# A log-softmax over rows of 50000: one product per tile in place of four, and a subtraction shared by two engines

## The chip, the cores and the metric

The kernel runs on one core of a Trainium2 chip. A core has a matrix engine (TensorE, PE in the profile), a vector engine (VectorE, DVE), a scalar engine (ScalarE, ACT), GpSimd (POOL) and SyncE (SP), which only issues transfers here. Sixteen DMA engines move data between the core's on-chip memory and the chip's main memory; their transfers are issued from SP (loads) and from ScalarE's queue (stores). The metric is the device time of one execution in microseconds (us), the median of several.

## What is computed

```python
batch, seq, vocab = 16, 512, 50000
max_x = np.max(x, axis=-1, keepdims=True)
shifted = x - max_x
log_sum_exp = np.log(np.sum(np.exp(shifted), axis=-1, keepdims=True))
return (shifted - log_sum_exp).astype(np.float32)
```

There are 8192 rows of 50000 numbers in float32. Each row is read once and written once.

## The kernel before

A tile is 32 rows. Each row lies on four neighbouring partitions (`G = 4`), so a tile fills 128 partitions with 12500 columns each (`W`), 50000 bytes on a partition. There are 256 tiles and four buffers for them (`NBUF = 4`, `bufs`); tile t uses buffer t mod 4. A tile is read into its buffer, changed in place and stored from there. For some steps the columns are taken in four pieces of 3125 (`NS`, `C`, `cols(c)`).

The order of work is written out by hand, engine by engine, with semaphores between the engines. There is no scheduler. `Count` (L35 and on) numbers the events of a semaphore, and `take` (L47) waits for a transfer and lowers its semaphore again. Most tiles run in a hardware loop of four tiles a round, with the first and last four outside on VectorE and the last four outside on ScalarE and TensorE.

- SP loads. The first four tiles are loaded at once (the first in two halves). After that the load of tile t + 4 waits at `take` until the store of tile t has landed (L158 to L161).
- VectorE, for a tile: wait until it has landed (L201); four maxima over 3125 columns each, negated, into `negm` (L206); the smallest of the four, `negp` (L211); then `share`, two transposes with a reduction and a copy between them (L171 to L186), which makes the four partitions of a row agree on one maximum, `negmax`. When ScalarE has its scales, VectorE multiplies them with the four partial sums, `scaled` (L217), and, when the logarithm is there, it subtracts maximum and logarithm from the whole tile in place (L191). Only the last tile is subtracted in four pieces.
- ScalarE, for a tile: after each of the four maxima, the exponential of that piece with its own maximum, summed into `part` (L248), the exponentials themselves being thrown away in `dump`; the four scales that bring the partial sums to the common maximum (L256); the logarithm of the row sum (L239); and then the issue of the tile's store, which waits until VectorE has subtracted (L243). Behind a store on this queue stand the next tile's exponentials. The last tile is stored in four pieces (L278 and L279).
- TensorE adds up: four products of the constant matrix `ones` (1 where two partitions belong to the same row) with the four columns of `scaled`, accumulated into one column of `sums` (L285).

In short, for one tile: load, maxima (with the exponentials behind them), agreement, scales, `scaled`, products, logarithm, subtraction, store.

Of the kernel before, what the change touches and what calls it, by code (L numbers as in the profile page):

```python
# [9 lines left out]
ACT = mybir.ActivationFunctionType  # L10
ALU = mybir.AluOpType
AX = mybir.AxisListType.X
# [6 lines left out]
C = 3125  # L19
NBUF = 4  # L20

NS = 4

HEAD = 2

# [19 lines left out]
def take(engine, sem, n=16):  # L45

    engine.wait_ge(sem, n).then_inc(sem, -n)  # L47


def cols(c):  # L50
    return slice(c * C, (c + 1) * C)
# [3 lines left out]
def kernel(  # L55
# [9 lines left out]
    W = V // G  # L65
    assert N % R == 0 and W == NS * C
    ntiles = N // R
# [6 lines left out]
    ot = of.rearrange("(t r) (g w) -> t (r g) w", r=R, g=G)  # L74

    def run(a, first, n):

        part = a[first : first + NBUF * n].rearrange("(q i) p w -> q i p w", i=NBUF)
        return lambda q, i: part[bass.ds(q, 1), i].rearrange("o p w -> (o p) w")
# [12 lines left out]
    ones = consts.tile([P, P], FP32, name="ones")  # L92
    bufs = [data.tile([P, W], FP32, name=f"buf{j}") for j in range(NBUF)]
    dump = dump_pool.tile([P, C], FP32, name="dump")
    sums = sum_pool.tile([P, NBUF], FP32, name="sums")
    rowsums = [sums[:, k : k + 1] for k in range(NBUF)]

    def each(n, width, name):
        return [stats.tile([P, width], FP32, name=f"{name}{j}") for j in range(n)]

    negms, parts, scales, scaleds = (
        each(NBUF, NS, n) for n in ("negm", "part", "scale", "scaled")
    )
    negmaxs, logs = each(NBUF, SQ, "negmax"), each(NBUF, 1, "logsum")
    (negp,) = each(1, 1, "negp")
    (allneg,) = each(1, SQ, "allneg")
    (rowneg,) = each(1, SQ // G, "rowneg")
# [5 lines left out]
    def sem(name):  # L113
        return ctx.enter_context(nc.semaphore(name))

    landed = [sem(f"landed{j}") for j in range(NBUF)]
    stored = [sem(f"stored{j}") for j in range(NBUF)]
    heads = [sem(f"head{h}") for h in range(HEAD)]
    ready = sem("ones_ready")
    on_dve = Count(sem("on_dve"))  # L120
    on_act = Count(sem("on_act"))
    shifted = Count(sem("shifted"))
    agreed = Count(sem("agreed"))
    rescaled = Count(sem("rescaled"))
    summed = Count(sem("summed"))
    added = Count(sem("added"))
    logged = Count(sem("logged"))
    subtracted = Count(sem("subtracted"))

    block = ctx.enter_context(nc.Block())  # L130

    @block.gpsimd
    def _(gpsimd):
        view = ones.rearrange("p (r g) -> p r g", g=G)
        gpsimd.memset(ones, 1.0).then_inc(ready)  # L135
        gpsimd.affine_select(  # L136
            out=view, in_=view, pattern=[[-G, R], [0, G]], base=0,
            channel_multiplier=1, compare_op=ALU.is_ge, fill=0.0,
        ).wait_op(ready, 1, "sem-ge").then_inc(ready)
        gpsimd.affine_select(  # L140
            out=view, in_=view, pattern=[[G, R], [0, G]], base=G - 1,
            channel_multiplier=-1, compare_op=ALU.is_ge, fill=0.0,
        ).wait_op(ready, 2, "sem-ge").then_inc(ready)

    @block.sync
    def _(sync):
# [15 lines left out]
        for j in range(NBUF - 1):  # L162
            take(sync, stored[j])
        take(sync, stored[NBUF - 1], 16 * NS)

    @block.vector
    def _(vector):
        def share(k):

            on_dve.next(  # L170
                vector.transpose(out=allneg, in_=negp.to_broadcast([P, SQ]))  # L171
            ).then_inc(on_dve.sem)
            on_dve.next(
                vector.tensor_reduce(  # L174
                    out=rowneg, in_=allneg.rearrange("p (r g) -> p r g", g=G),
                    op=ALU.min, axis=AX,
                )
            ).then_inc(on_dve.sem)
            on_dve.next(
                vector.tensor_copy(  # L180
                    out=spread.rearrange("p (r g) -> p r g", g=G),
                    in_=rowneg[:, :, None].to_broadcast([P, SQ // G, G]),
                )
            ).then_inc(on_dve.sem)
            on_dve.next(
                vector.transpose(out=negmaxs[k], in_=spread)  # L186
            ).then_inc(agreed.sem)

        def subtract(k, *bufs):
            for n, buf in enumerate(bufs):  # L190
                ins = vector.tensor_scalar(  # L191
                    out=buf, in0=buf, scalar1=negmaxs[k][:, 0:1], scalar2=logs[k],
                    op0=ALU.add, op1=ALU.subtract,
                )
                if n == 0:
                    logged.next(ins)
                ins.then_inc(subtracted.sem)

        def whole(j, first=False, by_pieces=False):
            if not first:  # L200
                take(vector, landed[j])  # L201

            for c in range(NS):
                if first and c % (NS // HEAD) == 0:
                    take(vector, heads[c // (NS // HEAD)])
                vector.tensor_reduce(  # L206
                    out=negms[j][:, c : c + 1], in_=bufs[j][:, cols(c)],
                    op=ALU.max, axis=AX, negate=True,
                ).then_inc(shifted.sem if c < NS - 1 else on_dve.sem)
            on_dve.next(vector.nop()).then_inc(shifted.sem)  # L210
            vector.tensor_reduce(  # L211
                out=negp, in_=negms[j], op=ALU.min, axis=AX
            ).then_inc(on_dve.sem)
            share(j)

            rescaled.next(
                vector.tensor_mul(out=scaleds[j], in0=scales[j], in1=parts[j])  # L217
            ).then_inc(summed.sem)
            subtract(j, *([bufs[j][:, cols(c)] for c in range(NS)] if by_pieces else [bufs[j]]))

        def settle():
            for count in (on_dve, rescaled, logged):
                count.settle(vector)

        for j in range(NBUF):
            whole(j, first=j == 0)
        settle()
        with vector.Fori(0, rounds - 1):
            for j in range(NBUF):
                whole(j)  # L230
            settle()
        for j in range(NBUF):
            whole(j, by_pieces=j == NBUF - 1)

    @block.scalar
    def _(scalar):
        def log(k):
            added.next(
                scalar.activation(out=logs[k], in_=rowsums[k], func=ACT.Ln)  # L239
            ).then_inc(logged.sem)  # L240

        def store(j, dst, buf):
            subtracted.next(scalar.dma_start(out=dst, in_=buf)).then_inc(stored[j], 16)  # L243

        def whole(j):
            for c in range(NS):
                shifted.next(
                    scalar.activation(  # L248
                        out=dump, in_=bufs[j][:, cols(c)], func=ACT.Exp,
                        bias=negms[j][:, c : c + 1], scale=1.0,  # L250
                        accum_out=parts[j][:, c : c + 1],
                    )
                ).then_inc(on_act.sem)
                on_act.next(scalar.nop())  # L254
            agreed.next(
                scalar.activation(  # L256
                    out=scales[j], in_=negms[j], func=ACT.Exp,
                    bias=negmaxs[j][:, 0:1], scale=-1.0,
                )
            ).then_inc(rescaled.sem)  # L260
            log(j)

        def settle():
            for count in (on_act, shifted, agreed, added, subtracted):
                count.settle(scalar)

        nc.scalar.preload_act_table_set("natural_log_exp_and_others")  # L267
        dst = run(ot, 0, rounds)
        with scalar.Fori(0, rounds) as q:
            for j in range(NBUF):  # L270
                whole(j)
                store(j, dst(q, j), bufs[j])
            settle()
        for j in range(NBUF - 1):
            whole(j)
            store(j, ot[ntiles - NBUF + j], bufs[j])
        whole(NBUF - 1)
        for c in range(NS):  # L278
            store(NBUF - 1, ot[ntiles - 1][:, cols(c)], bufs[NBUF - 1][:, cols(c)])  # L279

    @block.tensor
    def _(tensor):
        def whole(j):
            for c in range(NS):
                ins = tensor.matmul(  # L285
                    rowsums[j], ones, scaleds[j][:, c : c + 1],
                    start=c == 0, stop=c == NS - 1,
                )
                if c == 0:
                    summed.next(ins)  # L290
            ins.then_inc(added.sem)

        tensor.wait_ge(ready, 3)
        with tensor.Fori(0, rounds):
            for j in range(NBUF):
                whole(j)
            summed.settle(tensor)
        for j in range(NBUF):
            whole(j)
# [30 lines left out]
```

## Time and profile before

| what | value |
|---|---|
| median of 3 runs | 7586.61 us (7581.52 to 7590.15) |
| the profiled execution's own time | 7610.41 us |
| its span in the profile | 7608.7 us |
| VectorE busy | 5441.5 us, 72% |
| ScalarE busy | 3184.7 us, 42% |
| TensorE busy | 477.9 us, 6% (2048 records) |
| bytes moved | 3276.85 MB, mean 431 GB/s |
| maximum over 3125 columns (L206), 1024 of them | 3401 ns each |
| exponential over 3125 columns (L248), 1024 of them | 2868 ns each |
| subtraction over 12500 columns (L191) | 6791 ns each |
| product of `scaled` (L217), 128x4 | 163 ns each |
| minimum of four columns (L211), 128x4 | 157 ns each |
| load of a tile, 6250 KB, issue to landing | 44.2 us, median |
| store of a tile, 6250 KB, issue to landing | 47.9 us, median |

An engine's busy time leaves out its waits and the issue of transfers. One product of `ones` with a column of float32 appears as two records of weights and two of the product itself, hence 2048 records for 256 x 4 products. The busy times of the engines overlap in time, so they are not to be added.

### The profile page before, as it was taken

The page shows a single profiled execution, that of the slowest core. Times are in us where ns is not written, and L with a number is a line of the kernel's source. Part 1 is how long each engine was busy: PE and PEld are TensorE (multiplying, and loading weights), DVE is VectorE, ACT ScalarE, POOL GpSimd, SP SyncE. Part 2 cuts the span into 40 slices and gives each one's busy share as a digit, 9 for nine tenths or more (in the row PEclk, how much of TensorE's full clock was granted, in tenths as well). Part 3 has the DMA queues.
Part 4 walks back from the last instruction along what each step waited for, and adds up shares of the span by engine and source line. Part 5 has one row for each costly group of instructions (what it writes and reads, how often), then busy time and mean ns, then how long its engine had stood idle before and what let it go on. Part 6 is the DMA issues. An engine that isn't in the chain of part 4 may idle for free. (4 is left out here: it accounts for less than half of the span.)

```text
span 7608.7 us, 14069 instructions
## 1 busy us (share of the span) xinstructions
PE 477.9 (6%) x2048; PEld 456.0 (6%) x2048; DVE 5441.5 (72%) x2819; ACT 3184.7 (42%) x2561; POOL 1.4 (0%) x7
## 2 busy tenths in 40 slices
PE   0000000000000000000000000000000000000000
PEld 0000000000000000000000000000000000000000
DVE  7777777767777777777777777777777777777776
ACT  4444443443434444344443444434344443443443
POOL 0000000000000000000000000000000000000000
DMA  9999999999999999999999999999999999999999
GB/s 425 435 434 433 433 432 433 432 430 433 435 434 433 433 432 431 433 433 433 433 431 433 433 432 432 433 430 433 431 432 433 430 432 427 430 428 430 431 429 387
DMA packets 74307, 3276.85 MB, mean 431 GB/s; under 512 B 8257, under 2 KB 8257, under 8 KB 8257
## 3 DMA queue, kind: packets, MB, share of 16 engines
q1 hardware_dynamic: 37008, 1638.42, 50.2%
q10 hardware_dynamic: 37296, 1638.42, 49.8%
q14 instruction: 3, 0.02, 0.0%
HBM read 1638.40 MB, written 1638.40 MB: 431 GB/s over the span
## 5 line engine op out<-in xcount | busy, mean ns | idle before, releaser
L248 ACT ACTIVATE dump<-buf,negm 128x3125 f32<-128x3125 f32 x1024 | 2937.3, 2868 | 3828.4 <-DVE negm L206 3730.9
L206 DVE TENSOR_REDUCE negm<-buf 128x1 f32<-128x3125 f32 x1024 | 3418.4, 3401 | 946.4 <-DVEq L47 946.4
L191 DVE TENSOR_SCALAR buf<-buf,negmax,logsum 128x12500 f32<-128x12500 f32 (+1 forms) x259 | 1739.0, 6715 | 553.7 <-ACT logsum L239 553.7
L285 PE MATMUL sums<-scaled,ones 128*128 128x1 f32 x2048 | 477.9, 355 | 7110.7 <-DVE scaled L217 7110.7
L285 PEld LDWEIGHTS sums<-scaled,ones 128*128 128x128 f32 x2048 | 456.0, 328 | 7132.6 <-DVE scaled L217 7132.6
L217 DVE TENSOR_TENSOR scaled<-scale,part 128x4 f32<-128x4 f32 x256 | 41.7, 163 | 579.9 <-ACT scale L256 579.9
L239 ACT ACTIVATE logsum<-sums 128x1 f32<-128x1 f32 x256 | 43.8, 171 | 551.1 <-PE sums L285 551.1
L248 ACT ACTIVATION_READ_ACCUMULATOR dump<-buf,negm 128x1 f32 x1024 | 190.9, 186 | 0.0
L256 ACT ACTIVATE scale<-negm,negmax 128x4 f32<-128x4 f32 x256 | 76.1, 297 | 23.6
L211 DVE TENSOR_REDUCE negp<-negm 128x1 f32<-128x4 f32 x256 | 40.2, 157 | 39.2 <-DVE negm L206 39.2
L186 DVE STREAM_TRANSPOSE negmax<-spread 128x32 f32<-128x32 f32 x256 | 54.2, 212 | 8.9
L171 DVE STREAM_TRANSPOSE allneg<-negp 128x32 f32<-128x32 f32 x256 | 54.2, 212 | 8.9
L174 DVE TENSOR_REDUCE rowneg<-allneg 128x8 f32<-128x32 f32 x256 | 47.7, 186 | 8.9
L180 DVE COPY spread<-rowneg 128x32 f32<-128x32 f32 x256 | 46.5, 182 | 8.9
L267 ACT ACT_TABLE_LOAD x1 | 1.3, 1283 | 1.0 <-SPq L111 1.0
L136 POOL TENSOR_SCALAR_AFFINE_SELECT ones<-ones 128x128 f32<-128x128 f32 x1 | 0.5, 518 | 0.1
L140 POOL TENSOR_SCALAR_AFFINE_SELECT ones<-ones 128x128 f32<-128x128 f32 x1 | 0.5, 517 | 0.1
L135 POOL MEMSET ones<- 128x128 f32 x1 | 0.2, 204 | 0.5 <-SPq L111 0.5
L314 POOL MEMSET const-bfloat16-1.0<- 128x1 bf16 x1 | 0.1, 101 | 0.0
L314 POOL MEMSET const-uint8-127<- 128x1 uint8 x1 | 0.1, 101 | 0.0
L314 POOL MEMSET const-float32-0.0<- 128x1 f32 x1 | 0.1, 98 | 0.3 <-issue 0.3
L314 POOL MEMSET const-float32-1.0<- 128x1 f32 x1 | 0.1, 98 | 0.0
## 6 DMA issues: line engine op xcount, KB each, us to landing
buf<-in_x_dram SPq DMA_DIRECT2D x255, 6250.0 KB, 44.2
out_dram<-buf ACTq DMA_DIRECT2D x255, 6250.0 KB, 47.9
buf<-in_x_dram SPq DMA_DIRECT2D x2, 3125.0 KB, 14.0
out_dram<-buf ACTq DMA_DIRECT2D x4, 1562.5 KB, 8.1
```

Source lines behind the costliest of these rows:

```text
L171: vector.transpose(out=allneg, in_=negp.to_broadcast([P, SQ]))
L174: vector.tensor_reduce(out=rowneg, in_=allneg.rearrange("p (r g) -> p r g", g=G), op=ALU.min, axis=AX,)
L180: vector.tensor_copy(out=spread.rearrange("p (r g) -> p r g", g=G), in_=rowneg[:, :, None].to_broadcast([P, SQ // G, G]),)
L186: vector.transpose(out=negmaxs[k], in_=spread)
L191: ins = vector.tensor_scalar(out=buf, in0=buf, scalar1=negmaxs[k][:, 0:1], scalar2=logs[k], op0=ALU.add, op1=ALU.subtract,)
L206: vector.tensor_reduce(out=negms[j][:, c : c + 1], in_=bufs[j][:, cols(c)], op=ALU.max, axis=AX, negate=True,).then_inc(shifted.sem if c < ...
L211: vector.tensor_reduce(out=negp, in_=negms[j], op=ALU.min, axis=AX).then_inc(on_dve.sem)
L217: vector.tensor_mul(out=scaleds[j], in0=scales[j], in1=parts[j])
L239: scalar.activation(out=logs[k], in_=rowsums[k], func=ACT.Ln)
L248: scalar.activation(out=dump, in_=bufs[j][:, cols(c)], func=ACT.Exp, bias=negms[j][:, c : c + 1], scale=1.0, accum_out=parts[j][:, c : c + 1],
L256: scalar.activation(out=scales[j], in_=negms[j], func=ACT.Exp, bias=negmaxs[j][:, 0:1], scale=-1.0,)
L285: ins = tensor.matmul(rowsums[j], ones, scaleds[j][:, c : c + 1], start=c == 0, stop=c == NS - 1,)
```

## The change

TensorE's four products per tile become one: VectorE first adds the four columns of `scaled` into one column, `totals`, and that is multiplied with `ones`. The subtraction of a tile is divided by columns. VectorE subtracts the first three quarters (9375 columns, `OWN`) as before. For the last quarter VectorE computes `offsets`, the negated maximum less the logarithm, in one column, and ScalarE adds it to the last 3125 columns in place with an Identity activation whose bias is that column. The store of a tile now waits for both: a no-operation on ScalarE waits for its own Identity, and the store itself for VectorE. On the last tile VectorE subtracts three pieces, and the four stores wait one by one for their own piece, the fourth for the Identity. The full diff but for the new counters and lists:

```diff
+OWN = (NS - 1) * C
...
+    totals = each(NBUF, 1, "total")
+    offsets = each(NBUF, 1, "offset")
...
+    offset = Count(sem("offset"))
+    shared = Count(sem("shared"))
...
         def subtract(k, *bufs):
-            for n, buf in enumerate(bufs):
-                ins = vector.tensor_scalar(
+            logged.next(
+                vector.tensor_sub(out=offsets[k], in0=negmaxs[k][:, 0:1], in1=logs[k])
+            ).then_inc(offset.sem)
+            for buf in bufs:
+                vector.tensor_scalar(
                     out=buf, in0=buf, scalar1=negmaxs[k][:, 0:1], scalar2=logs[k],
                     op0=ALU.add, op1=ALU.subtract,
-                )
-                if n == 0:
-                    logged.next(ins)
-                ins.then_inc(subtracted.sem)
+                ).then_inc(subtracted.sem)
...
             rescaled.next(
                 vector.tensor_mul(out=scaleds[j], in0=scales[j], in1=parts[j])
+            ).then_inc(on_dve.sem)
+            on_dve.next(
+                vector.tensor_reduce(
+                    out=totals[j], in_=scaleds[j], op=ALU.add, axis=AX
+                )
             ).then_inc(summed.sem)
-            subtract(j, *([bufs[j][:, cols(c)] for c in range(NS)] if by_pieces else [bufs[j]]))
+            own = [cols(c) for c in range(NS - 1)] if by_pieces else [slice(0, OWN)]
+            subtract(j, *(bufs[j][:, part] for part in own))
...
         def store(j, dst, buf):
+            shared.next(scalar.nop())
             subtracted.next(scalar.dma_start(out=dst, in_=buf)).then_inc(stored[j], 16)
...
             log(j)
+            offset.next(
+                scalar.activation(
+                    out=bufs[j][:, OWN:], in_=bufs[j][:, OWN:], func=ACT.Identity,
+                    bias=offsets[j], scale=1.0,
+                )
+            ).then_inc(shared.sem)
...
         for c in range(NS):
-            store(NBUF - 1, ot[ntiles - 1][:, cols(c)], bufs[NBUF - 1][:, cols(c)])
+            count = shared if c == NS - 1 else subtracted
+            count.next(
+                scalar.dma_start(
+                    out=ot[ntiles - 1][:, cols(c)], in_=bufs[NBUF - 1][:, cols(c)]
+                )
+            ).then_inc(stored[NBUF - 1], 16)
...
         def whole(j):
-            for c in range(NS):
-                ins = tensor.matmul(
-                    rowsums[j], ones, scaleds[j][:, c : c + 1],
-                    start=c == 0, stop=c == NS - 1,
-                )
-                if c == 0:
-                    summed.next(ins)
-            ins.then_inc(added.sem)
+            summed.next(
+                tensor.matmul(rowsums[j], ones, totals[j], start=True, stop=True)
+            ).then_inc(added.sem)
```

## The prediction

> **What bounds the kernel now.** I read first the page's slices, because they say whether any engine or the DMA engines are full all the way; then the waits, to see who is late; then one tile of the timeline; then the end of the span in windows.
>
> The page, its slices (each a fortieth of the span, 190 us) and its queues:
>
> ```profile
> span 7608.7 us, 14069 instructions
> DVE  7777777767777777777777777777777777777776
> ACT  4444443443434444344443444434344443443443
> DMA  9999999999999999999999999999999999999999
> GB/s 425 435 434 433 433 432 433 432 430 433 435 434 433 433 432 431 433 433 433 433 431 433 433 432 432 433 430 433 431 432 433 430 432 427 430 428 430 431 429 387
> q1 hardware_dynamic: 37008, 1638.42, 50.2%
> q10 hardware_dynamic: 37296, 1638.42, 49.8%
> ```
>
> VectorE is busy seven tenths of the time, ScalarE four. The two DMA queues, loads (q1) and stores (q10), take 50.2% and 49.8% of 16 engines' time: together all of it. The rate is flat at 427 to 435 GB/s from the second slice to the last but one; only the ends drop. The work is 3276.85 MB, which no edit of the change touches.
>
> The list of waits (who waited for whom: us in total, times, longest):
>
> ```profile
> ACT dump L248 <- DVE negm L206: 3730.9, 768, 15.3
> DVE negm L206 <- DVEq L47: 946.4, 253, 11.7
> DVE scaled L217 <- ACT scale L256: 579.9, 256, 2.3
> DVE buf L191 <- ACT logsum L239: 553.7, 256, 2.2
> ```
>
> The second line decides. L47 is `take`, VectorE's wait for a tile to land, and it came last 253 times of 256. The engines wait for data; they are not what data waits for. One tile of the timeline (start, duration, engine, work, idle before it and releaser):
>
> ```profile
> 7527.32 0.16 DVE L217 TENSOR_TENSOR scaled<-scale,part 128x4 f32<-128x4 f32 x1 [2.26 <-ACT scale L256]
> 7527.53 1.87 PE L285 MATMUL sums<-scaled,ones 128*128 128x1 f32 x8 [27.64 <-DVE scaled L217]
> 7529.44 0.17 ACT L239 ACTIVATE logsum<-sums 128x1 f32<-128x1 f32 x1 [2.15 <-PE sums L285]
> 7529.64 6.79 DVE L191 TENSOR_SCALAR buf<-buf,negmax,logsum 128x12500 f32<-128x12500 f32 x1 [2.16 <-ACT logsum L239]
> 7536.47 0.35 ACTq L243 DMA_DIRECT2D out_dram<-buf  x1
> 7539.97 3.41 DVE L206 TENSOR_REDUCE negm<-buf 128x1 f32<-128x3125 f32 x1 [3.53 <-DVEq L47]
> ```
>
> After its store is issued VectorE stands idle 3.53 us. The next tile's subtraction begins at 7559.15 in the same view, 29.51 us after this one. A tile moves 6250 KB each way, 12.8 MB; at 433 GB/s that is 29.56 us. So the period is the DMA's, and the compute of a tile is 29.51 - 3.53 = 26.0 us of it.
>
> The end, in windows (us, busy time of PE, its weight load, DVE, ACT and POOL, clock, DMA share of 16 engines, GB/s):
>
> ```profile
> 7500.00:7558.00 58.00, 2.83 (x13) 2.74 (x13) 42.51 (x22) 24.80 (x20) 0.00 (x0) 1.00 1.00 429
> 7567.00:7580.00 13.00, 0.00 (x0) 0.00 (x0) 10.30 (x4) 6.21 (x5) 0.00 (x0) 1.00 1.00 431
> 7582.00:7590.00 8.00, 1.87 (x8) 1.78 (x8) 3.28 (x8) 4.22 (x6) 0.00 (x0) 1.00 0.06 25
> 7592.00:7606.00 14.00, 0.00 (x0) 0.00 (x0) 4.24 (x3) 0.00 (x0) 0.00 (x0) 1.00 1.02 429
> ```
>
> The share of 0.06 is one engine of sixteen. One DMA engine lags behind the others and is still storing tile 254 while the rest idle before tile 255's pieces, whose first store is issued at 7590.82. It has hardly a gap of its own, so it sets the end.
>
> **What the Trainium skill says.** "DMA: Bandwidth & Descriptors", section "Where 436 GB/s comes from", puts the ceiling of a core's 16 DMA engines at 435.2 GB/s; the page's 430 to 435 agrees, there is nothing left above it. "SBUF — State Buffer", section "Who interferes with whom", says that DMA never contends with a compute engine. The trace agrees as far as it can: 13 us with only stores and a busy VectorE ran at 431 GB/s, 14 us with VectorE mostly idle at 429. "ScalarE: Activation LUTs", section "What ACT_TABLE_LOAD costs", gives 280 ns + 0.833 ns an element for an ACTIVATE with a bias of one value per partition, whatever the function: 2883 ns for 3125 columns; the exponential of that width takes 2868 here. "VectorE: DVE Perf Modes", section "Mode 2×_2P — use both read ports for one tensor", allows two elements a cycle for an odd width if source and destination have the same; the trace has such an odd case, the last tile's 3125 columns at about 1.9 us, against 3.4 us for a maximum over as many.
>
> **The change part by part.** Times are per tile, from the product on VectorE (L217) on.
>
> Products: the eight PE records of a tile take 1.87 us, of 355 ns each by the page, so their starts lie (1.87 - 0.355) / 7 = 0.22 us apart. Two remain: 0.22 + 0.355 = 0.57 us. Gain 1.30.
>
> New sum over four columns (`totals`): nearest row the minimum over four columns at L211, 157 ns, and about 0.03 us of start. Cost 0.19; bounds 0.16 and 0.25.
>
> New `offsets`: a 128x1 subtraction, nearest row L217's 163 ns, plus 0.03 between instructions. It stands on VectorE ahead of the large subtraction. Cost 0.2; bounds 0.1 and 0.25.
>
> Large subtraction: 12500 columns take 6.79 us, 3125 take 1.84 (7.36 over four). Between them (6.79 - 1.84) / 9375 = 0.528 ns a column, so 9375 columns take 1.84 + 6250 x 0.528 = 5.14 us. Gain 1.65. If the odd width fell to one element a cycle, at the maximum's 3.4 us per 3125 it would be about 10.2 us: a loss of 3.4.
>
> ScalarE's Identity on 3125 columns: 2.87 us, bounds 2.8 and 3.3, since it writes to SBUF where the exponential writes to PSUM. It begins when the offset is there, beside VectorE's 5.14 us, so it ends some 2.2 us before and hides. Behind it on ScalarE stand the new no-operation that waits for it, the store, and the next tile's exponentials, which could not start sooner than a landing and a maximum later anyway. SP's loads wait only for stores.
>
> Sum: the chain from landing to store loses 1.30 + 1.65 - 0.19 - 0.2 = 2.56 us, 26.0 to 23.4. Over 256 tiles that is 655 us of compute taken away, and none of it lies on the path: the next tile has not landed. VectorE's wait at `take` grows from 3.5 to about 6.1 us, in total from 946 to 946 + 253 x 2.56 = about 1590 us. The store enters a DMA queue earlier and stays in it that much longer. The first loop rounds, where tiles follow without a wait at L47, gain nothing either: DMA is full from 2.2 us on (426 GB/s up to 60 us).
>
> Only the end is not covered by DMA. There the last tile's first piece is issued earlier by 1.30 - 0.19 - 0.2 = 0.9 us, provided that its DMA issue passes the Identity that runs ahead of it on ScalarE; if it doesn't, the issue follows Identity, 2.87 instead of 1.9 us after the offset, and the net is nothing. The later three pieces have a DMA engine to wait for in either case. And the lagging engine is busy with tile 254 until about 7591.6, so a gain stops at about 0.7. I take 0.5.
>
> Against the profiled execution: 7610.4 (span 7608.7 and 1.7 outside it) - 0.5 = 7609.9. The median of the timed runs is 24 us lower, 0.3%, and nothing in the profile says why; the same 0.5 makes it 7586.
>
> **The rivals.**
> - The shorter chain shortens the loop. A buffer's cycle is 44.2 (load) + 26.0 + 47.9 (store) = 118.1 us by the page's medians, four periods. If latency ruled, 2.56 us in 64 rounds would be 164 us, time 7423. Against: it needs 12.8 MB in 28.9 us, 443 GB/s, above every slice. What remains is a better DMA rate by different timing: 434 for the 432.0 that slices 2 to 39 average is 0.5%, 35 us, 7552. Nothing in the change asks for it.
> - The DMA rate falls (the slower side). The place is the interleaving of loads and stores on the 16 engines: the rate sinks from 432.9 (slices 2 to 20) to 429.2 (34 to 39), at the time the lagging engine shows. Stores that enter earlier could let the engines drift apart from the start. At 429.2 throughout it is 7636: 3276.85 MB / 429.2 = 7635 against 7586 at 432.0, 49 us more. It decides from 0.2%, a mean of 431.1. For it: the drift is in this very trace. Against: the queues are already full, and nobody stops an engine that has work.
> - The change doesn't do what it says: the odd 9375 columns run at one element a cycle. Chain 26.0 + 2.5 = 28.5 us, still under 29.5; the time stays 7586 to 7590 and only the last tile feels it, which keeps its 3125-wide pieces anyway.
> - Compute becomes the bound: it takes a chain over 29.5 us, an Identity of more than 11 us in place of 2.87. I give it no share.
>
> **How the numbers follow.** A measurement of this kernel can tell about 0.2%, 15 us. No change (the forecast, with both variants of the tail and the odd width) 0.87; a higher DMA rate, faster, 0.05; a lower one, slower, 0.08. The forecast's own spread is the tail's 0 to 0.9 us and the runs' 7581.5 to 7590.2. To hold 8 in 10 with a different chip and some drift I take 7571 to 7605.
>
> **What would show it.** Right: DMA at 9 in all slices, 430 to 435 GB/s; PE near 150 us; DVE near 5440 - 255 x 1.65 + 256 x 0.32 = 5100; ACT near 3185 + 256 x 2.87 = 3920; the wait at `take` near 6 us a tile. Wrong: a subtraction over 5.5 us, an Identity that ends after VectorE's part, slices under 428, or VectorE's wait for landings unchanged. The prediction fails if the DMA rate moves by more than 0.2%, since the time is bytes over that rate plus some 20 us at the ends.

## The result, and the profile after

The changed kernel took 7639.52 us, median of 5 runs (7622.72 to 7649.55), against 7586.61 (7581.52 to 7590.87) for the kernel before: a ratio of 1.0064, 95% interval 1.0040 to 1.0088. It is 53 us slower, outside the range of the forecast and close to the time of its slower rival, 7636. The profiled execution took 7633.4 us. The ratios here and below leave out executions more than 1.5% above the fastest of their kernel (two of e3, seven of e10) and are not those of the medians, so that the two can differ a little.

The page of the changed kernel, its busy times, slices (190.8 us each) and queues:

```profile
span 7631.7 us, 11893 instructions
PE 150.2 (2%) x512; PEld 128.3 (2%) x512; DVE 5083.0 (67%) x3330; ACT 3927.0 (51%) x2817; POOL 1.4 (0%) x7
DMA  9999999999999999999999999999999999999998
GB/s 424 434 432 435 432 434 433 435 433 433 433 432 435 432 435 432 435 433 432 434 432 433 433 432 431 427 430 427 429 427 428 424 425 427 428 427 427 428 426 377
q1 hardware_dynamic: 37008, 1638.42, 50.2%
q10 hardware_dynamic: 37296, 1638.42, 49.7%
```

The engines do less, as they should. The DMA row still shows 9 up to the last slice, and still the rate steps down: slices 2 to 25 average 433.1 GB/s, slices 26 to 39 average 427.1. Those 14 slices are 2671 us, and 2671 x (1 - 427.1 / 433.1) = 37 us. The last slice adds to it: 377 GB/s. The kernel before had 387 there and a smaller, later drop (429.2 in slices 34 to 39).

The list of waits of the changed kernel:

```profile
ACT dump L260 <- DVE negm L211: 3235.0, 768, 13.4
DVE negm L211 <- DVEq L48: 1645.1, 256, 11.5
DVE offset L196 <- ACT logsum L250: 225.9, 256, 0.9
ACT buf L275 <- DVE offset L196: 58.1, 256, 0.2
```

The second line is the wait for a tile to land, 946 us before and 1645 now. VectorE gained 2.6 us a tile and spends them waiting. One tile of the timeline of the changed kernel:

```profile
7521.02 0.16 DVE L222 TENSOR_TENSOR scaled<-scale,part 128x4 f32<-128x4 f32 x1 [2.26 <-ACT scale L268]
7521.22 0.16 DVE L225 TENSOR_REDUCE total<-scaled 128x1 f32<-128x4 f32 x1
7521.43 0.58 PE L308 MATMUL sums<-total,ones 128*128 128x1 f32 x2 [29.43 <-DVE total L225]
7522.05 0.17 ACT L250 ACTIVATE logsum<-sums 128x1 f32<-128x1 f32 x1 [1.06 <-PE sums L308]
7522.25 0.16 DVE L196 TENSOR_TENSOR offset<-negmax,logsum 128x1 f32<-128x1 f32 x1 [0.88 <-ACT logsum L250]
7522.33 5.16 DVE L199 TENSOR_SCALAR buf<-buf,negmax,logsum 128x9375 f32<-128x9375 f32 x1
7522.45 2.90 ACT L275 ACTIVATE buf<-buf,offset 128x3125 f32<-128x3125 f32 x1 [0.23 <-DVE offset L196]
7527.52 0.35 ACTq L255 DMA_DIRECT2D out_dram<-buf  x1
7533.88 13.35 DVE L211 TENSOR_REDUCE negm<-buf 128x1 f32<-128x3125 f32 x4 [6.39 <-DVEq L48]
```

From `scaled` to the issue of the store it takes 7527.52 - 7521.02 = 6.50 us, where the kernel before took 7536.47 - 7527.32 = 9.15. VectorE then stands idle for 6.39 us instead of 3.53. The 16 us from the last tile's first store on, in the changed kernel and in the kernel before (columns as in the prediction's windows):

```profile
7614.00:7630.00 16.00, 0.00 (x0) 0.00 (x0) 3.42 (x2) 0.90 (x1) 0.00 (x0) 1.00 0.95 400
...
7591.00:7607.00 16.00, 0.00 (x0) 0.00 (x0) 5.24 (x3) 0.00 (x0) 0.00 (x0) 1.00 0.95 400
```

These stores are as fast as before: from the first of them to the end of the span it is 17.9 us in both (7613.81 to 7631.7, and 7590.82 to 7608.7). The end loses its time ahead of them. The last load is complete on 15 of the 16 DMA engines at 7570.8 us and on the last one at 7593.6, 22.8 us later; in the kernel before it was 7557.0 and 7569.6, 12.6 us. The lag of one engine, for which the last tile has to wait, has grown by 10 us.

So the question is what an earlier store does to the rate of transfers that, by the busy share, have no idle time to lose.

**Inside the transfers.** The trace also holds the single packets. A row's packet (50000 bytes) takes 1.847 us in most cases and hardly ever less, and each of the 16 DMA engines carries 16 of them per tile, 8 in and 8 out, so 16 x 1.847 = 29.55 us, the period. The landings of one transfer on its 16 engines show how far these have drifted apart. In the changed kernel the last engine lands 3 us after the first at 300 us, 11 us at 2700, and from 4500 us on 25 to 30 us, nearly a whole period; late in the run it is one engine that is 23 us behind the other fifteen. The pace is 29.5 to 29.8 us a tile up to 4700 us and 29.9 to 30.1 after that. The shares of the two queues show what this does. First two windows at 2504 to 2512 us and 2519 to 2527 us of the changed kernel (queue, packets, MB, share of 16 engines), on either side of a store's issue at 2512.3 (loads were issued at 2500.1 and 2529.6):

```profile
q10 hardware_dynamic: 42, 2.10, 60.6%
q1 hardware_dynamic: 35, 1.20, 34.7%
...
q1 hardware_dynamic: 34, 1.70, 49.1%
q10 hardware_dynamic: 35, 1.55, 44.8%
```

Then the same places of the period late in the run, 6530 to 6538 us and 6545 to 6553 us (loads issued at 6526.1 and 6556.1, a store at 6538.3):

```profile
q1 hardware_dynamic: 64, 3.20, 92.4%
q10 hardware_dynamic: 6, 0.10, 2.9%
...
q10 hardware_dynamic: 61, 3.05, 88.0%
q1 hardware_dynamic: 21, 0.30, 8.8%
```

Early, loads and stores share the engines in both windows. Late they take turns: most engines have emptied one queue before its next transfer is issued, so nearly all carry loads at once, then stores at once. The Trainium skill, "DMA: Bandwidth & Descriptors", section "Queues, rings and completion order", says that an engine goes round-robin between the queues it has work for, packet by packet. The early windows agree, as far as shares over 8 us can; with one queue empty there is nothing to alternate with, which is what the late ones show. In this late stretch (5500 to 7300 us) the packets of loads take on average 90 to 400 ns more than 1.847 us from 1 to 4 us after a load or a store has been issued, and mostly under 40 ns more in between. Stores slow far less: they have 4.6 of the 47 us that the longer packets add up to, per DMA engine, from 200 to 7400 us. A longer packet is a busy engine, so the DMA row cannot show it.

How many engines have run a queue empty can be counted from the landings: at each issue of a load or a store, take the engines that have already finished the transfer ahead of it in its queue. In the changed kernel it is none of the 16 from 2000 to 3000 us, at 434 GB/s; 10 or 11 from 3700 to 4600, still at 433; and 15 from 5500 to 7000, at 427.

### The profile page after: what moved, and what is told of

Its sections match the earlier page's. It is cut to its first block, busy times and chain, and to the rows that moved or that the text cites. A ratio compares the mean times of both kernels' runs of the same rounds, so it can differ in the third digit from the quotient of the medians.

```text
span 7631.7 us, 11893 instructions
## 1 busy us (share of the span) xinstructions
PE 150.2 (2%) x512; PEld 128.3 (2%) x512; DVE 5083.0 (67%) x3330; ACT 3927.0 (51%) x2817; POOL 1.4 (0%) x7
## 3 DMA queue, kind: packets, MB, share of 16 engines
q1 hardware_dynamic: 37008, 1638.42, 50.2%
## 5 line engine op out<-in xcount | busy, mean ns | idle before, releaser
L199 DVE TENSOR_SCALAR buf<-buf,negmax,logsum 128x9375 f32<-128x9375 f32 (+1 forms) x258 | 1320.4, 5118 | 0.0
L275 ACT ACTIVATE buf<-buf,offset 128x3125 f32<-128x3125 f32 x256 | 742.3, 2900 | 58.1 <-DVE offset L196 58.1
L308 PE MATMUL sums<-total,ones 128*128 128x1 f32 x512 | 150.2, 362 | 7461.4 <-DVE total L225 7461.4
L308 PEld LDWEIGHTS sums<-total,ones 128*128 128x128 f32 x512 | 128.3, 311 | 7483.1 <-DVE total L225 7483.1
L196 DVE TENSOR_TENSOR offset<-negmax,logsum 128x1 f32<-128x1 f32 x256 | 40.8, 160 | 225.9 <-ACT logsum L250 225.9
L268 ACT ACTIVATE scale<-negm,negmax 128x4 f32<-128x4 f32 x256 | 76.1, 297 | 23.6
L225 DVE TENSOR_REDUCE total<-scaled 128x1 f32<-128x4 f32 x256 | 40.3, 157 | 8.8
```

The source lines that it names most:

```text
L199: vector.tensor_scalar(out=buf, in0=buf, scalar1=negmaxs[k][:, 0:1], scalar2=logs[k], op0=ALU.add, op1=ALU.subtract,).then_inc(subtracted.sem)
L268: scalar.activation(out=scales[j], in_=negms[j], func=ACT.Exp, bias=negmaxs[j][:, 0:1], scale=-1.0,)
L275: scalar.activation(out=bufs[j][:, OWN:], in_=bufs[j][:, OWN:], func=ACT.Identity, bias=offsets[j], scale=1.0,)
L308: tensor.matmul(rowsums[j], ones, totals[j], start=True, stop=True)
```

## The experiments

Times are medians over 3 or 5 rounds, and ratios are to the kernel before, run on the same chip in the same rounds: 7580.90 us for the first four, 7585.20 for the next four, 7585.68, 7584.17 (e12) and 7585.48 us after that. The chain is from the start of a tile's first maximum to the issue of its store. The extra is how much longer than 1.847 us the row packets took, from 200 to 7400 us of the profiled execution, in sum and per DMA engine.

| run | chain, us | time, us | ratio (95%) | extra, us |
|---|---|---|---|---|
| before (e1 to e4's) | 26.0 | 7580.90 | 1 | 30 |
| after, once more (e4) | 23.4 | 7638.21 | 1.0066 (1.0049 to 1.0083) | 50 |
| e1, delay to 25.9 | 25.9 | 7593.77 | 1.0014 (1.0006 to 1.0023) | 16 |
| e2, share alone | 24.5 | 7672.51 | 1.0132 (1.0103 to 1.0161) | 87 |
| e3, product alone | 24.9 | 7667.91 | 1.0090 (1.0061 to 1.0120) | 73 |
| e5, delay to 24.5 | 24.5 | 7667.04 | 1.0116 (1.0093 to 1.0140) | 73 |
| e6, delay to 27.0 | 27.0 | 7585.94 | 1.0002 (0.9994 to 1.0010) | 9 |
| e7, one drain | 23.4 | 7602.72 | 1.0037 (1.0016 to 1.0057) | 25 |
| e8, no load behind a load | 23.4 | 7850.67 | 1.0333 (1.0301 to 1.0366) | 208 |
| e9, after, first load whole | 23.4 | 7625 to 8526 | none | 60 |
| e10, share, first load whole | 24.5 | 7638.28 | 1.0044 (1.0026 to 1.0062) | 92 |
| e11, before, first load whole | 26.0 | 7598.01 | 1.0025 (1.0011 to 1.0039) | 14 |
| e12, before in one queue | 26.2 | 7594.10 | 1.0014 (1.0007 to 1.0021) | 15 |
| e13, after in one queue | 23.6 | 7595.57 | 1.0014 (1.0007 to 1.0022) | 18 |
| e14, share in one queue | 24.7 | 7596.20 | 1.0015 (1.0008 to 1.0023) | 18 |

The line of before has the extra of its own earlier profile (7610.4 us). The extra is of one execution, which need not be near the median: that of e9 took 7635.8 us, that of e10 7683.9.

**e1, the changed kernel with its store put off.** VectorE takes a maximum that nobody uses over 2300 columns, 2.55 us, between the logarithm and `offsets`. All the change's instructions stay.

```diff
+DELAY = 2300
...
             logged.next(
+                vector.tensor_reduce(
+                    out=idle, in_=full[:, :DELAY], op=ALU.max, axis=AX
+                )
+            ).then_inc(on_dve.sem)
+            on_dve.next(
                 vector.tensor_sub(out=offsets[k], in0=negmaxs[k][:, 0:1], in1=logs[k])
```

> The whole change, plus one VectorE maximum over 2300 columns (about 2.5 us) between the logarithm and the offset, so that a tile's chain is again about 26 us and the stores enter their queue when they did before. Theory T (timing: the stores that come 2.6 us earlier set loads and stores in another position to each other, and the loads' packets slow down): 7580 to 7600, ratio to the kernel before under 1.002. Rival S (ScalarE's in-place subtraction itself disturbs the transfers): about 7640, ratio 1.004 to 1.009, as for the changed kernel.

7593.77 us: of the 57 us that the change lost on this chip (e4), 44 are back. Its slices and its wait for landings:

```profile
GB/s 426 434 434 434 434 433 433 434 433 433 432 433 433 434 433 431 433 434 433 434 434 433 433 434 434 434 434 434 434 432 433 433 433 431 431 431 430 432 431 380
...
DVE negm L219 <- DVEq L50: 950.0, 254, 11.6
```

The wait is 950 us, as before the change, and the rate stays at 431 to 434 from slice 2 to slice 36. So neither the Identity, nor the sum, nor the single product costs the time. The moment at which the store is issued does, with the work just ahead of it, which the delay moves too.

**e2, the share without the single product.** The changed kernel with the four products of before.

```diff
-            summed.next(
-                tensor.matmul(rowsums[j], ones, totals[j], start=True, stop=True)
-            ).then_inc(added.sem)
+            for c in range(NS):
+                ins = tensor.matmul(
+                    rowsums[j], ones, scaleds[j][:, c : c + 1],
...
```

> ScalarE takes the last quarter of the subtraction, four products stay; the chain is about 1.4 us shorter than before. Theory T: something between, ratio 1.000 to 1.006, since the stores come earlier by half as much. Rival S: the full loss, ratio 1.004 to 1.009.

7672.51 us, 92 us lost where the whole change lost 57, with a store only 1.6 us earlier than before. Its slices:

```profile
GB/s 425 433 433 432 432 432 432 431 432 429 433 433 432 434 431 430 427 430 429 427 425 428 427 426 429 426 429 427 427 427 425 428 426 427 427 427 422 413 426 372
```

**e3, the single product without the share.** The kernel before with `totals` and one product; VectorE subtracts the whole tile.

```diff
+            on_dve.next(
+                vector.tensor_reduce(
+                    out=totals[j], in_=scaleds[j], op=ALU.add, axis=AX
+                )
             ).then_inc(summed.sem)
...
+            summed.next(
+                tensor.matmul(rowsums[j], ones, totals[j], start=True, stop=True)
+            ).then_inc(added.sem)
```

> One product with the sum on VectorE, VectorE subtracts alone; the chain is about 1.1 us shorter than before. Theory T: something between, ratio 1.000 to 1.006, nearly as for the share alone. Rival S: no change, ratio 0.999 to 1.001.

7667.91 us, from 7577 to 7704 over ten runs. ScalarE does nothing new here, and the loss is there all the same, but for one of the ten, the 7577. Its slices:

```profile
GB/s 426 434 434 433 434 433 434 434 434 433 434 433 434 434 434 434 433 434 431 434 434 434 432 433 434 432 434 423 417 421 422 421 417 423 415 420 420 418 418 379
```

For 27 slices it runs as well as any kernel here, then it falls within two slices, to 415 to 423, and stays there. What this execution lost, it lost in a state that the transfers entered at some time, not a little per tile. Up to 4500 us no engine has run a queue empty when the next transfer is issued; after the fall 14 have.

**e4, the changed kernel again**, as the measure for these.

> The changed kernel as it is, for comparison on the same chip. Both theories: ratio 1.004 to 1.009 as in the first measurement. If it comes out under 1.002 on this chip, the loss belongs to the chip or the placement of the data and not to the change.

7638.21 us, ratio 1.0066: the first result stands.

**e5 and e6, other delays.** e1 with 900 columns and with 3350 in place of 2300.

```diff
-DELAY = 2300
+DELAY = 900
```

> The whole change with an extra VectorE maximum over 900 columns (about 1.1 us) on the chain: 24.5 us, as long as with the share alone. Theory T in its first form (the longer the chain, the later the stores, the nearer to before): between the changed kernel and before, ratio 1.001 to 1.006. Its refinement P (what counts is the place of a store's issue between two load issues, 11.2 us after a load in the kernel before, 12.2 in the changed one, 13.3 with the share alone): if the place is again near 13.3, worse than the change, ratio 1.008 to 1.016.

> The whole change with a maximum over 3350 columns (about 3.65 us): the chain is 27.1 us, longer than before. First form of T: no loss, ratio 0.999 to 1.0015. P: the place of the store is near 12.3 us after a load as in the changed kernel, and the loss is back, ratio 1.003 to 1.009.

e5 took 7667.04 us. Its chain, 24.5 us, is that of e2, and so is its loss, though e5 has the one product and e2 the four. e6 took 7585.94, no loss at all. Slices of e6:

```profile
GB/s 426 433 434 432 434 432 434 432 433 434 435 433 432 434 434 435 433 433 434 435 434 432 434 434 433 433 432 433 434 433 433 434 432 433 434 432 434 431 434 397
```

The loss is not monotone in the chain: 23.4 us loses 0.7%, 24.5 to 24.9 lose 0.9 to 1.3%, 25.9 and 27.0 lose 0.1 and nothing. Nor does one place of the store after the load decide it. The store of e6 moves from about 8.5 to about 11.2 us behind the load's issue and keeps its rate; that of e3 lies at 10.1 us both while its rate holds and after it has fallen.

**e7, the changed kernel drained once.** After 40 rounds of the loop (tile 164) SP waits until all four stores have landed and then issues four loads. The work is otherwise the same.

```diff
+        with sync.Fori(0, DRAIN) as q:
...
+        for j in range(NBUF):
+            take(sync, stored[j])
+        for j in range(NBUF):
+            load(j, src(DRAIN, j))
+        with sync.Fori(DRAIN + 1, rounds) as q:
```

> The whole change; after 164 of the 256 tiles SP waits once until all four buffers are stored, then loads four. Theory D (the slow stretch is a state: the DMA engines have drifted apart until the leaders run out of queued work): after the drain, near 4900 us, the slices go back from 427 to 432 or more GB/s for at least 1000 us, and the landings of one transfer lie within 5 us again; the time is 7590 to 7640. Rival A (the later tiles are slow by where their data lie): slices stay near 427 after the drain and the time is 15 to 40 us above the changed kernel's.

7602.72 us (15 runs, 7594 to 7703, two of them over 7650): slower than before, but 0.4% instead of 0.7, the price of the drain included. Its slices:

```profile
DMA  9999999999999999999999999899999999999999
GB/s 424 430 432 434 433 433 433 432 433 434 432 433 433 432 431 429 431 429 432 429 433 430 431 432 432 379 433 433 435 434 433 433 433 433 435 434 433 433 433 421
```

The drain is the 379, and after it 433 to 435 hold to the end, where the undrained kernel ran at 427. The spread of a store's landings is 22 us ahead of the drain, then 2.2 to 3.3 us, and the pace 29.54 us a tile; no engine runs a queue empty any more before the next issue. The tiles after it have the same chain, the same addresses and the same buffers. So the slow stretch is not a matter of which tiles they are; it is a state of the transfers, and it ended with the drain. The drain changed two things, though: it brought the engines together, and it moved the stores from 12.2 us behind a load's issue to within 1.2 us of one. This run doesn't tell which of the two counts. With the engines together at the end, the last slice has 421 GB/s instead of 377; that alone is (421 - 377) / 433 x 190 = 19 us.

**e8, no load queued behind a load.** SP's next load also waits until VectorE has seen the last one land.

```diff
             for j in range(NBUF):
+                take(sync, begun, 1)
                 take(sync, stored[j])
                 load(j, src(q, j))
...
+                vector.wait_ge(landed[j], 16).then_inc(begun, 1)
                 take(vector, landed[j])
```

> The whole change, but SP issues a load only when VectorE has seen the one before it land, so that the leading DMA engines cannot be more than one load ahead. Theory D: the spread of the landings stays small and no slow stretch comes, ratio 0.998 to 1.002. Rival: one queued load is too little and the engines starve, ratio above 1.01; or the spread is not what counts, ratio 1.004 to 1.009.

7850.67 us. This was to keep the engines together, and it did (landings within 1 to 3 us). Its slices:

```profile
DMA  9999999999999999999999999999999999999999
GB/s 422 414 412 413 417 412 418 419 417 412 419 421 418 417 414 410 419 418 412 423 414 423 417 418 414 419 418 422 416 415 425 423 421 416 410 415 416 411 412 390
```

The rate is 410 to 425 all the way under a row of nines. So a small spread doesn't keep the rate. Here every engine has run its load queue empty when the next load is issued, and loads and stores are slow together (extra 106 and 102 us). From 200 to 7400 us the engines are busy for a share of 0.99, where every other two-queue run has 1.00.

**e9, e10, e11, the first tile loaded whole.** If a drained start keeps the engines together, loading tile 0 at once instead of in halves might do it from the beginning. One edit to the changed kernel (e9), to e2 (e10) and to the kernel before (e11):

```diff
-HEAD = 2
+HEAD = 1
```

> The whole change, and the first tile is loaded in one transfer, not in two halves, so that the first store comes about 6 us later against the loads, as it did after the drain. Theory M (what costs is that loads and stores of all DMA engines come in turns, all loads and then all stores; the opening sets the place of stores between loads, and the drain set a good one): stores are issued within 2 us of a load issue for the whole run, slices stay at 432 or more, the landings of one transfer lie within 6 us, ratio 0.997 to 1.0005. Rival (the good stretch after the drain came of the drain itself, or of too little time left to drift): the loss stays, ratio 1.004 to 1.009.

> The share alone with its four products, the slowest of the first runs (ratio 1.013), with the first tile loaded whole. Theory M: the place of the stores is another from the start, and with it the loss; a ratio that differs from 1.010 to 1.016 by more than 0.005. Rival: as before, 1.010 to 1.016.

> The kernel before with the first tile loaded whole. Theory M: the place of its stores moves from 11.2 us after a load and the time with it, in a direction that I can't tell, ratio 0.997 to 1.012; it is 11.2 us again and the ratio 1.000 if the opening doesn't set the place. Rival: ratio 0.999 to 1.001 in any case.

It is no cure. Four of the six executions of e9 took 8478 to 8526 us and two took 7626 and 7636. The profile is of one of the latter, so where those 0.85 ms went is open, and no ratio is taken. e10 took 7638.28 (median of executions from 7576 to 8278), e11 7598.01, slower than before by 0.25%. So one chain can take different times with a different start, and with the same start too.

e9 and e10 also bear on what the changed kernel's trace suggests. The slices of e9, then of e10, and two windows of e9, 3500 to 3508 us and 3516 to 3524 us:

```profile
GB/s 426 433 432 434 431 432 431 433 431 432 431 431 430 429 429 431 428 430 427 423 428 428 428 431 429 428 430 430 428 431 430 428 431 431 431 431 431 430 431 400
...
GB/s 420 434 434 434 433 433 433 434 433 434 435 433 433 433 434 433 433 434 433 433 431 426 422 420 424 422 423 422 422 421 422 419 419 420 421 423 424 422 423 379
...
q10 hardware_dynamic: 41, 2.05, 59.2%
q1 hardware_dynamic: 37, 1.40, 40.5%
...
q1 hardware_dynamic: 33, 1.65, 50.2%
q10 hardware_dynamic: 35, 1.65, 47.6%
```

e10 falls to 422 while the landings of a transfer lie only 14 us apart, half a period, and 13 engines have then run a queue empty, none before the fall. e9 sinks to 428 with none, and with loads and stores mixed in its windows: turns between the queues are not needed for a loss. Up to 1300 us its stores are issued within 1.3 us of a load's issue, where those of e7 are after the drain; by 1700 us they have moved to 4.5 us, so starting at this place isn't enough to stay there and keep the rate.

**e12, e13, e14, loads and stores in one queue.** SP issues the stores too, by turns with the loads: the store of tile n + 1, then the load of tile n + 4. ScalarE issues nothing. e12 is the compute of before, e13 of after, e14 of e2.

```diff
+        def store(j, dst, buf):
+            take(sync, subtracted.sem, 1)
+            sync.dma_start(out=dst, in_=buf).then_inc(stored[j], 16)
+
+        store(0, ot[0], bufs[0])
         with sync.Fori(0, rounds) as q:
             for j in range(NBUF):
+                k = (j + 1) % NBUF
+                store(k, dst(q, j), bufs[k])
                 take(sync, stored[j])
                 load(j, src(q, j))
```

> The kernel before, with its compute unchanged; SP issues the stores too, in one queue with the loads, a store of a tile and a load of another by turns, so that every DMA engine moves eight rows one way and then eight the other, and none can mix them. Theory M (loads and stores by turns cost, mixed row by row they don't): DMA at 9 in all slices and yet a rate of 420 to 429 GB/s from early on, ratio 1.008 to 1.03. Rival (turns cost nothing; the slow stretch has another cause): 432 to 434 GB/s, ratio 0.998 to 1.003.

> The whole change, with loads and stores in SP's one queue by turns, as in e12. Theory Q (the loss arises between the two queues, when the leading DMA engines have run one of them dry; the change only moved the stores there): rate 433 throughout, ratio 1.000 to 1.003, the same as e12 within 0.001, so the change itself costs nothing. Rival (an earlier store or ScalarE's part costs in any arrangement of the queues): slower than e12 by 0.004 or more.

> The share alone with four products (ratio 1.013 with two queues, the slowest of the parts), in one queue. Theory Q: as e12 and e13, ratio 1.000 to 1.003. Rival: 1.008 or more.

7594.10, 7595.57 and 7596.20 us, each 0.14 or 0.15% above before. Over all 52 runs they lie between 7592.9 and 7600.0. The page of e12:

```profile
GB/s 424 430 434 433 433 432 434 433 433 432 433 433 433 432 433 433 433 433 433 433 433 433 433 433 433 433 433 433 432 434 433 434 432 433 433 434 433 433 434 387
q1 hardware_dynamic: 74304, 3276.83, 99.9%
```

All rows go through q1, a tile out and a tile in by turns, and the rate is 432 to 434 to the last slice but one. So turns as such cost nothing. From 500 to 7300 us no engine has run its queue empty at any issue, in all three runs. Three things changed at once, however: the queue, the engine that issues the stores, and the order of loads and stores, which is now fixed. Which of them ends the loss was not tried. The page and the waits of e13:

```profile
GB/s 423 430 432 432 432 432 432 433 432 433 433 432 434 433 432 434 433 433 433 434 433 433 433 433 434 432 433 433 433 433 433 433 433 433 433 433 433 433 432 398
...
DVE negm L228 <- DVEq L48: 1596.7, 254, 11.2
```

The shorter chain is there (1597 us of waits, where the prediction had 1590), and the 0.7 to 1.3% that shorter chains lost in two queues is gone. In one queue the chain makes a difference of about 2 us at most.

No version was faster than the kernel before beyond the spread of its runs.

## Why the prediction was wrong

**Right: every step of the compute.** The product: 0.62 us from its start to the logarithm (7521.43 to 7522.05) where it was 1.91, a gain of 1.29; 1.30 was predicted. The sum: 0.21 us, 0.19 predicted. The large subtraction: 5.16 us, 5.14 predicted, so the rival of one element a cycle falls. The Identity: 2.90 us, 2.87 predicted, and it ends at 7525.35, 2.1 us ahead of VectorE's part. `offsets` was put at 0.2 us and costs 0.08, since the subtraction starts 0.08 us after it. In sum 2.65 us a tile, 2.56 predicted. VectorE is busy 5083 us (about 5100 predicted), TensorE 150, ScalarE 3927 (3920). That the next tile has not landed, so that none of the gain reaches the end, is also right.

**Right: the store of the last tile passes the Identity.** It is issued at 7613.81, 2.0 us after the offset, while the Identity runs until 7614.90. The 0.5 us that this was to bring can't be seen beside what the lag of the engines costs at the end.

**Wrong: "The store enters a DMA queue earlier and stays in it that much longer".** The prediction costed this at nothing, and named full DMA queues as the cover; it cost 53 us. e1 and e6 show that this step is the loss: with all of the change and a later store, 7593.77 and 7585.94 us. The reverse holds too: e2 and e3 lose with half of the change, and e5 loses with a store 1.5 us earlier than before, not 2.6. The cover was judged from the DMA row and the shares of the queues, 50.2% and 49.8%. These say that an engine has a packet in hand, not how long the packet takes. A row took 1.847 us in good stretches and, for some microseconds of each period, 0.1 to 0.4 us more in bad ones (up to 0.6 in e3), and both read as 9.

**The rival that came true.** "The DMA rate falls" had the place (the interleaving of loads and stores on the 16 engines), the sign in the trace of before (433 sinking to 429) and the size: a mean of 429.2 gave 7636, and the page after shows a mean of 429 and 7639.5. What was set against it, "the queues are already full, and nobody stops an engine that has work", is refuted: e3 ends at 415 to 423 GB/s with 9 in every slice. That the size came so near is partly luck. The rival had a constant 429.2; the trace has 433.1 up to slice 25, then 427.1, and a slower end. The prediction named slices under 428 as a sign of being wrong, and so it was, but one slice of the kernel before, the 34th, reads 427 already.

**What is shown and what is not.** Shown by runs: the loss follows the moment of the store (e1, e2, e3, e5, e6), not ScalarE's or TensorE's work, and the start has a part in it (e10); it is a state that ended with a drain (e7); it is absent where SP issues loads and stores by turns into one queue (e12 to e14). The skill's statement that DMA doesn't contend with a compute engine, "SBUF — State Buffer", section "Who interferes with whom", agrees with e13, which has ScalarE's writes and e12's time.

Shown by the traces as a sum: from 200 to 7400 us the engines are never idle in the changed kernel or in e1 to e6 (share 1.00), so what they lose there is what their packets take longer. The extra goes with the profiled executions' own times (e6 9 us and 7584.3; e1 16 and 7598.7; e5 73 and 7661.7; e2 87 and 7676.6): of the 92 us between e6 and e2 it is 78.

Only correlated: that packets are slow after a transfer arrives in a queue that most engines have run empty. The slow stretches of the changed kernel and of e2, e3, e5 and e10 have 12 to 15 such engines on average, e6 and the one-queue runs none or nearly none; 11 or 12 need not cost much (the kernel before had them from 4000 to 5500 us, at 432 GB/s); e8, which made all 16 run the load queue empty, was the slowest. But e9 lost without any, and no experiment set the count by itself. Why such a packet takes longer, why the engines drift apart, why 23.4 us loses less than 24.5, what slowed e9 and the 0.14% of the one queue remain open.

## What to carry to other kernels

In a kernel that waits for its transfers, a shorter chain of compute gains nothing by itself, and here it wasn't free: it moved the issue of stores against that of loads. Read the rate by slices of the span and not the busy share, and compare packet times, because an engine with a slow packet is as busy as one with a fast one. Look in the landings, too, for engines that have run a queue empty before its next transfer is issued. The small drift in the rate of the kernel before was a warning that the balance depends on timing; putting loads and stores into one queue, by turns, took that dependence away here, for 0.14%.

## What the runs showed of the hardware beside that

- The 16 engines of one transfer do not stay together: with loads and stores of equal rows, one engine was 23 us behind the other fifteen by 6000 us. In one queue it was 9 us behind by 7400 (e13).
- The lag costs a second time at the end, where the others have nothing left: the last slice had 377 GB/s with a lag of 23 us and 421 with the engines within 5 us (e7).
- Between two states of the transfers there can be a sharp step. e3 went from 434 to 417 GB/s within two slices, in the middle of a loop whose rounds are all alike; e10 went from 433 to 422 within three.
